# Output weights, input row norms and first convolution tap: a change of engine and of order in a gated DeltaNet and MLA kernel

## The chip, the cores and the metric

The kernel runs on one core of one Trainium2 chip. The metric is the device time of one execution in microseconds (us). Of several executions the median counts; two kernels are compared by executions that alternate on the same chip.

## What is computed

The reference is a streaming encoder with two layers. Layer A is a gated DeltaNet, layer B a latent attention (MLA). 1024 tokens of width 1024 come in, 16 meta tokens are put ahead of them, and both layers have 8 heads of width 128. The change touches layer A alone:

```python
def deltanet_layer(x, valid, g_norm, w_in, conv_w, a_log, dt_bias, o_gain, w_out):
    h = jnp.where(valid[None, :, None], rms_norm(x, g_norm), 0)
    z = h @ w_in
    qkv = jax.nn.silu(causal_dwconv(z[..., :2 * DN_KW + DN_VW], conv_w))   # 4 taps for each channel
    gate = z[..., 2 * DN_KW + DN_VW:2 * DN_KW + 2 * DN_VW]
...
    o = gated_delta_rule(to_chunks(q), to_chunks(k), to_chunks(v), gate_chunks(g), gate_chunks(beta))
    o = o.transpose(0, 2, 3, 1, 4).reshape(bsz, lp, DN_HEADS, DN_DV)
    o = rms_norm(o, o_gain) * jax.nn.silu(gate).reshape(bsz, lp, DN_HEADS, DN_DV)
    return x + o.reshape(bsz, lp, DN_VW) @ w_out
```

Shared keys and values, the attention layer and its output projection follow; they stay as they are.

## The kernel before

All products are split: an operand is rounded to the matmul's reduced fp32 (`hi`), the remainder is kept (`lo`), and three products (hi hi, hi lo, lo hi; the helper `mm3`, lines 93 to 95) make one. So each operand needs a rounding and a remainder. `split_w` does that for weights: the rounding on GpSimd (line 100, or line 103 with a gain) or VectorE, the remainder on VectorE (lines 101 and 104). `split_ps` does it for PSUM, with the rounding on ScalarE (lines 109 and 112).

The 1040 tokens go through layer A in three chunks of 272, 384 and 384 columns (`TOKC`). The stages that matter here:

Input. The first chunk comes transposed from memory (`x0`). For the other two, three row tiles of 128 tokens each are loaded (`xt`), squared on ScalarE with a sum for each row (`tok_norms`, into row tiles `xs`, of which there are 4), scaled on GpSimd by the inverse norm (line 292), transposed by TensorE (line 297) and split into `hT_hi` and `hT_lo`. Chunk 1 is squared early; chunk 2 is squared, scaled and transposed in its turn of the loop.

Projections. `conv_acts` makes one head's keys, values or queries: for each chunk 24 products of a chunk's width into one of two PSUM banks (`mm`), a copy to `z` on ScalarE (line 389), the first tap on GpSimd (line 391), three taps on VectorE (line 394), a SiLU on ScalarE. That is 24 heads' parts by 3 chunks. The tile for values (`vT`) has one buffer, that for queries two, that for keys four. In between, `key_prep` transposes keys (line 416) and squares them on ScalarE out of PSUM, masks gate tiles on GpSimd (line 448) for TensorE (line 450), and `query_prep` makes one-column products (line 494) and key-query products (line 502). `invert_blocks` is a long run on VectorE (lines 543 and 546), and the chunk scan follows.

Gates and output weights. For each head h the gate projection (three chunks, a SiLU each on ScalarE, stored to `gt_scr` for the first six heads) and the output weights of that head: a raw tile (`raw`, two buffers) is loaded and split by line 743 with the gain `og` for each row. Beside it the output norms are raised to a power on GpSimd (line 712, `output_norms`). The projection weights of the last eight heads are rounded on VectorE.

Every engine and SyncE's queue of transfers runs its own list of instructions in order and waits on semaphores. The order in each list is settled when the program is built, by priority in program order and by what is ready then; it can differ from the order of the text.

Of the kernel before, what the change touches and what calls it, by code (L numbers as in the profile page):

```python
# [16 lines left out]
F32 = mybir.dt.float32  # L17
# [33 lines left out]
def tools(tc):  # L51
# [45 lines left out]
    def split_w(raw, hi, lo, gain=None, eng=G):  # L97

        if gain is None:
            eng.tensor_scalar(out=hi, in0=raw, scalar1=1.0, scalar2=1.0, op0=ALU.mult, op1=ALU.mult)  # L100
            V.tensor_tensor(out=lo, in0=raw, in1=hi, op=ALU.subtract)  # L101
        else:
            G.tensor_scalar(out=hi, in0=raw, scalar1=gain, scalar2=1.0, op0=ALU.mult, op1=ALU.mult)  # L103
            return V.scalar_tensor_tensor(out=lo, in0=raw, scalar=gain, in1=hi, op0=ALU.mult, op1=ALU.subtract)  # L104

    def split_ps(ps, hi, lo, gain=None):
# [12 lines left out]
def body(ctx: ExitStack, tc: tile.TileContext, I, out):  # L119
# [63 lines left out]
    with ExitStack() as la:  # L183
# [51 lines left out]
        with ExitStack() as l0:  # L235
# [19 lines left out]
            def tok_norms(tiles):  # L255

                ss = xp.tile([P, 3], F32, tag="ss", name=nm("ss"), bufs=2)
                xss = [xp.tile([P, D], F32, tag="xs", name=nm("xs"), bufs=4) for _ in tiles]
                for i, t in enumerate(tiles):
                    act(xss[i], xts[t], AF.Square, accum_out=ss[:, i:i + 1])  # L260
                rsqrt(ss, ss, 1.0 / D, EPS)
                return ss, xss


            ps = bank("tr", [P, 512])[:, 0:W0]
# [19 lines left out]
            ready[order[1]] = load_w(order[1])  # L285
            V.tensor_tensor(out=gg, in0=col("kg"), in1=col("qg"), op=ALU.mult)
            V.tensor_scalar(out=gg, in0=gg, scalar1=QK ** -0.5, scalar2=None, op0=ALU.mult)
            for c, (a, b) in list(enumerate(TOKC))[1:]:
                tiles = [t for t in range(NT) if a <= tok(t)[0] < b]
                ss, xss = first if c == 1 else tok_norms(tiles)  # L290
                for i, t in enumerate(tiles):
                    G.tensor_scalar(out=xss[i], in0=xts[t], scalar1=ss[:, i:i + 1], scalar2=1.0,
                                    op0=ALU.mult, op1=ALU.mult)
                for kt in range(KT):
                    ps = bank("tr", [P, 512])
                    for i, xs in enumerate(xss):
                        TE.transpose(ps[:, P * i:P * i + P], xs[:, kt * P:(kt + 1) * P], ident)
                    split_ps(ps[:, 0:b - a], hT_hi[:, kt, a:b], hT_lo[:, kt, a:b], col("a", kt))
# [82 lines left out]
        def conv_acts(c0, tag, bufs):  # L381

            hi, lo = weights(c0)
            m = c0 // P
            z = zp.tile([P, 3 + L], F32, tag="z", name=nm("z"))
            y = kp.tile([P, L], F32, tag=tag, name=nm(tag), bufs=bufs)
            G.memset(z[:, 0:3], 0.0)
            for c, (a, b) in enumerate(TOKC):
                A.copy(z[:, 3 + a:3 + b], gemm_T(hi, lo, c))  # L389
                yc = y[:, a:b]  # L390
                G.tensor_scalar(out=yc, in0=z[:, a:b], scalar1=col("cw", m), scalar2=1.0,  # L391
                                op0=ALU.mult, op1=ALU.mult)
                for j in range(1, 4):
                    V.scalar_tensor_tensor(out=yc, in0=z[:, a + j:b + j], scalar=col("cw", 24 * j + m), in1=yc,  # L394
                                           op0=ALU.mult, op1=ALU.add)
                act(yc, yc, AF.Silu)
            return y
# [334 lines left out]
        with ExitStack() as lr:  # L732
            rp = lr.enter_context(tpool(name="wr", bufs=2))
            for h in range(H):
# [5 lines left out]
                    SY.dma_start(gt_scr[h * P:(h + 1) * P, :], z)  # L740
                raw = rp.tile([P, D], F32, tag="raw", name=nm("raw"))
                SY.dma_start(raw, I["a_w_out"][0, h * P:(h + 1) * P, :])
                last = split_w(raw, w_hi[:, h, :], w_lo[:, h, :], col("og"))
                if h > 1:
                    next(norms, None)
            for _ in norms:
# [754 lines left out]
```

## Time and profile before

| | us |
|---|---|
| three executions | 1347.64, 1343.96, 1349.01 |
| their median | 1347.64 |
| the profiled execution, its own time | 1343.6 |
| its span, from first to last instruction | 1341.9 |
| TensorE products busy in it | 1299.7 |
| TensorE's mean granted clock | 0.992 |

A row of the profile names engines as PE (TensorE products), PEld (its weight loads), DVE (VectorE), ACT (ScalarE), POOL (GpSimd), SP (SyncE). L391 is line 391 of the kernel. An instruction's idle time is that of its engine just before it, and the name behind the arrow is what ended it. Ends of TensorE's products are modelled: a product of 384 columns is drawn as 0.34 us, and the next one starts 0.18 us after it.

### The profile page before, as it was taken

Reading aid. Unit: us, or ns where it says so; the run is one execution under the profiler, and the core shown is the slowest. Engines: PE = TensorE matmul, PEld = TensorE weight load, DVE = VectorE, ACT = ScalarE, POOL = GpSimd, SP = SyncE. Lnnn points to the kernel's source line nnn. Section 1 sums busy time; section 2 is a strip of 40 time slices with the busy share of each in tenths; the row PEclk is TensorE's granted clock in tenths of the full one; section 3 lists DMA queues with packets and bytes.
Section 4 is the critical chain, followed back from the end, with each engine's and each line's share of the span. In section 5 each row is a group of like instructions: output and inputs, shape, how many; then the busy total and the mean of one; then the engine's idle time right before and its main releaser. Section 6 shows DMA issues by size and latency. Waiting matters only on the chain.

```text
span 1341.9 us, 24805 instructions
## 1 busy us (share of the span) xinstructions
PE 1299.7 (97%) x9047; PEld 1178.1 (88%) x9047; DVE 901.2 (67%) x2588; ACT 533.0 (40%) x1680; POOL 405.9 (30%) x677
## 2 busy tenths in 40 slices
PE   6999999999999999999999999998999999999998
PEld 5879989989998999996888798887999999998787
DVE  6679779968988884634553765224888878878321
ACT  5432343234225322211232343116778677776200
POOL 3353224323431320060101402212535436337100
PEclk9999999999999999999999999999999999999999
DMA  5111202111211113255541303311111101014443
GB/s 195 32 33 40 57 20 62 41 42 31 66 50 31 50 32 97 68 168 175 160 137 65 95 1 91 115 48 57 42 41 33 58 21 37 20 38 136 143 145 110
DMA packets 91676, 96.81 MB, mean 72 GB/s; under 512 B 27422, under 2 KB 72414, under 8 KB 91554
## 3 DMA queue, kind: packets, MB, share of 16 engines
q1 hardware_dynamic: 91554, 95.23, 22.8%
q8 instruction: 71, 1.16, 0.4%
q14 instruction: 51, 0.42, 0.1%
HBM read 68.19 MB, written 27.01 MB: 71 GB/s over the span
## 4 chain that ended last, share of the span: by engine, by line
PE 71%; DVE 9%; issue 5%; POOL 5%; ACT 4%; DMA 3%; SPq 0%; ACTq 0%; DVEq 0%; POOLq 0%
PE sc L95 6%; PE sc L94 6%; PE sc L93 6%; PE mm L93 6%; PE mm L94 6%; PE mm L95 6%; PE bd L93 5%; PE bd L95 4%; PE bd L94 4%; PE pt L1331 2%; PE tr L502 1%; PE sc L1284 1%; PE sc L1285 1%; DVE qT L394 1%; PE po L95 1%
## 5 line engine op out<-in xcount | busy, mean ns | idle before, releaser
L93 PE MATMUL mm<-hT_hi,whi 128*128 128x384 f32 (+1 forms) x768 | 256.6, 334 | 6.8 <-ACT hT_hi L283 4.3
L94 PE MATMUL mm<-hT_lo,whi 128*128 128x384 f32 (+1 forms) x768 | 256.6, 334 | 0.5 <-DVE hT_lo L284 0.5
L95 PE MATMUL mm<-hT_hi,wlo 128*128 128x384 f32 (+1 forms) x768 | 255.3, 332 | 0.7 <-DVE wlo L101 0.7
L93 PEld LDWEIGHTS mm<-hT_hi,whi 128*128 128x128 f32 x768 | 147.4, 192 | 9.4 <-issue 7.8
L95 PEld LDWEIGHTS mm<-hT_hi,wlo 128*128 128x128 f32 x768 | 147.6, 192 | 2.3 <-DVE wlo L101 1.1
L94 PEld LDWEIGHTS mm<-hT_lo,whi 128*128 128x128 f32 x768 | 147.1, 192 | 2.5 <-DVE hT_lo L284 1.0
L110 DVE TENSOR_TENSOR pTl<-pt,pTh 128x256 fp32r<-128x256 f32 (+2 forms) x112 | 54.9, 494 | 11.9 <-ACT pTh L109 10.4
L100 POOL TENSOR_SCALAR whi<-raw 128x512 fp32r<-128x512 f32 x48 | 37.4, 792 | 76.9 <-PE mm L94 71.2
L84 ACT ACTIVATE P<-P,mx 128x144 f32<-128x144 f32 (+3 forms) x64 | 50.6, 791 | 21.7 <-DVE mx L1289 19.2
L93 PE MATMUL sc<-wo_hi,oTh 128*128 128x512 f32 (+1 forms) x144 | 57.6, 400 | 0.6 <-ACT oTh L777 0.6
L95 PE MATMUL sc<-wo_hi,oTl 128*128 128x512 f32 (+1 forms) x144 | 57.2, 397 | 0.0
L94 PE MATMUL sc<-wo_lo,oTh 128*128 128x512 f32 (+1 forms) x144 | 57.0, 396 | 0.0
L389 ACT COPY z<-mm 128x384 f32<-128x384 f32 (+1 forms) x72 | 31.8, 442 | 56.7 <-PE mm L95 56.7
L394 DVE SCALAR_TENSOR_TENSOR kn<-z,pcol,kn 128x384 f32<-128x384 f32 (+1 forms) x72 | 41.0, 572 | 18.6 <-POOL kn L391 17.9
L109 ACT CAST pTh<-pt 128x256 fp32r<-128x256 f32 (+2 forms) x112 | 47.2, 426 | 14.2 <-PE pt L1331 7.2
L1302 POOL TENSOR_SCALAR P<-P,sl 128x144 f32<-128x144 f32 (+3 forms) x64 | 51.5, 806 | 3.7
L1300 POOL TENSOR_SCALAR Pe<-P,sl 128x128 f32<-128x128 f32 x64 | 29.5, 462 | 71.3 <-DVE sl L1297 55.2
L95 PE MATMUL sc<-h_hi,wlo 128*128 128x512 f32 x128 | 50.8, 397 | 0.0
L94 PE MATMUL sc<-h_lo,whi 128*128 128x512 f32 x128 | 50.6, 396 | 0.0
L93 PE MATMUL sc<-h_hi,whi 128*128 128x512 f32 x128 | 50.5, 395 | 0.0
L101 DVE TENSOR_TENSOR wlo<-raw,whi 128x512 fp32r<-128x512 f32 x64 | 46.0, 730 | 6.6 <-POOL whi L100 6.5
L104 DVE SCALAR_TENSOR_TENSOR wlo<-raw,pcol,whi 128x128 fp32r<-128x128 f32 x64 | 23.4, 428 | 40.0 <-POOL whi L103 40.0
(390 smaller groups left out, 3953.2 us busy)
## 6 DMA issues: line engine op xcount, KB each, us to landing
raw<-in_a_w_in SPq DMA_DIRECT2D x64, 256.0 KB
xt<-in_x SPq DMA_DIRECT2D x14, 512.0 KB
o_scr<-o SPq DMA_DIRECT2D x64, 64.0 KB
raw<-in_a_w_out SPq DMA_DIRECT2D x8, 512.0 KB
on<-o_scr SPq DMA_DIRECT2D x8, 512.0 KB
x_scr<-xt SPq DMA_DIRECT2D x8, 512.0 KB
raw<-in_b_w_in SPq DMA_DIRECT2D x8, 512.0 KB
gb_scr<-z SPq DMA_DIRECT2D x8, 512.0 KB
```

The costliest lines, as they stand in the source:

```text
L84: i = A.activation(out_ap, in_ap, func, **kw)
L93: TE.matmul(ps, ahi, bhi, start=first, stop=False)
L94: TE.matmul(ps, ahi, blo, start=False, stop=False)
L95: TE.matmul(ps, alo, bhi, start=False, stop=last)
L100: eng.tensor_scalar(out=hi, in0=raw, scalar1=1.0, scalar2=1.0, op0=ALU.mult, op1=ALU.mult)
L101: V.tensor_tensor(out=lo, in0=raw, in1=hi, op=ALU.subtract)
L109: A.copy(hi, ps)
L110: V.tensor_tensor(out=lo, in0=ps, in1=hi, op=ALU.subtract)
L389: A.copy(z[:, 3 + a:3 + b], gemm_T(hi, lo, c))
L394: V.scalar_tensor_tensor(out=yc, in0=z[:, a + j:b + j], scalar=col("cw", 24 * j + m), in1=yc, op0=ALU.mult, op1=ALU.add)
L1300: G.tensor_scalar(out=Pe, in0=Pm[:, None, 0:NM].broadcast_to([P, E8, NM]), scalar1=s, scalar2=1.0, op0=ALU.mult, op1=ALU.mult)
L1302: G.tensor_scalar(out=Pm[:, 0:n], in0=Pm[:, 0:n], scalar1=s, scalar2=1.0, op0=ALU.mult, op1=ALU.mult)
```

## The change

Three edits. `split_w` with a gain takes the engine that it is given: the eight output weight tiles are rounded by ScalarE (`A.mul` with the gain as a scale for each partition) in place of GpSimd; the remainder stays on VectorE, and other callers with a gain keep GpSimd. The norms and the scaling of both later input chunks are issued ahead of the loop over their transposes, with 6 row tiles in place of 4. The first tap of the convolution is an `A.mul` on ScalarE in place of a multiplication on GpSimd.

```diff
--- before.py
+++ after.py
@@ -100,7 +100,10 @@
             eng.tensor_scalar(out=hi, in0=raw, scalar1=1.0, scalar2=1.0, op0=ALU.mult, op1=ALU.mult)
             V.tensor_tensor(out=lo, in0=raw, in1=hi, op=ALU.subtract)
         else:
-            G.tensor_scalar(out=hi, in0=raw, scalar1=gain, scalar2=1.0, op0=ALU.mult, op1=ALU.mult)
+            if eng is A:
+                A.mul(hi, raw, gain)
+            else:
+                G.tensor_scalar(out=hi, in0=raw, scalar1=gain, scalar2=1.0, op0=ALU.mult, op1=ALU.mult)
             return V.scalar_tensor_tensor(out=lo, in0=raw, scalar=gain, in1=hi, op0=ALU.mult, op1=ALU.subtract)
 
     def split_ps(ps, hi, lo, gain=None):
@@ -255,11 +258,17 @@
             def tok_norms(tiles):
 
                 ss = xp.tile([P, 3], F32, tag="ss", name=nm("ss"), bufs=2)
-                xss = [xp.tile([P, D], F32, tag="xs", name=nm("xs"), bufs=4) for _ in tiles]
+                xss = [xp.tile([P, D], F32, tag="xs", name=nm("xs"), bufs=6) for _ in tiles]
                 for i, t in enumerate(tiles):
                     act(xss[i], xts[t], AF.Square, accum_out=ss[:, i:i + 1])
                 rsqrt(ss, ss, 1.0 / D, EPS)
                 return ss, xss
+
+            def scaled(tiles, ss, xss):
+                for i, t in enumerate(tiles):
+                    G.tensor_scalar(out=xss[i], in0=xts[t], scalar1=ss[:, i:i + 1], scalar2=1.0,
+                                    op0=ALU.mult, op1=ALU.mult)
+                return xss
 
 
             ps = bank("tr", [P, 512])[:, 0:W0]
@@ -285,12 +294,9 @@
             ready[order[1]] = load_w(order[1])
             V.tensor_tensor(out=gg, in0=col("kg"), in1=col("qg"), op=ALU.mult)
             V.tensor_scalar(out=gg, in0=gg, scalar1=QK ** -0.5, scalar2=None, op0=ALU.mult)
+            rows = {1: scaled(range(2, 5), *first), 2: scaled(range(5, 8), *tok_norms(range(5, 8)))}
             for c, (a, b) in list(enumerate(TOKC))[1:]:
-                tiles = [t for t in range(NT) if a <= tok(t)[0] < b]
-                ss, xss = first if c == 1 else tok_norms(tiles)
-                for i, t in enumerate(tiles):
-                    G.tensor_scalar(out=xss[i], in0=xts[t], scalar1=ss[:, i:i + 1], scalar2=1.0,
-                                    op0=ALU.mult, op1=ALU.mult)
+                xss = rows[c]
                 for kt in range(KT):
                     ps = bank("tr", [P, 512])
                     for i, xs in enumerate(xss):
@@ -388,8 +394,7 @@
             for c, (a, b) in enumerate(TOKC):
                 A.copy(z[:, 3 + a:3 + b], gemm_T(hi, lo, c))
                 yc = y[:, a:b]
-                G.tensor_scalar(out=yc, in0=z[:, a:b], scalar1=col("cw", m), scalar2=1.0,
-                                op0=ALU.mult, op1=ALU.mult)
+                A.mul(yc, z[:, a:b], col("cw", m))
                 for j in range(1, 4):
                     V.scalar_tensor_tensor(out=yc, in0=z[:, a + j:b + j], scalar=col("cw", 24 * j + m), in1=yc,
                                            op0=ALU.mult, op1=ALU.add)
@@ -740,7 +745,7 @@
                     SY.dma_start(gt_scr[h * P:(h + 1) * P, :], z)
                 raw = rp.tile([P, D], F32, tag="raw", name=nm("raw"))
                 SY.dma_start(raw, I["a_w_out"][0, h * P:(h + 1) * P, :])
-                last = split_w(raw, w_hi[:, h, :], w_lo[:, h, :], col("og"))
+                last = split_w(raw, w_hi[:, h, :], w_lo[:, h, :], col("og"), A)
                 if h > 1:
                     next(norms, None)
             for _ in norms:
```

## Rows read from the trace of the kernel before

**Rows 1.** The page's first part: busy time of each engine over the whole span, its share, and the count of its instructions; PE is TensorE's products, PEld its weight loads.

```profile
PE 1299.7 (97%) x9047; PEld 1178.1 (88%) x9047; DVE 901.2 (67%) x2588; ACT 533.0 (40%) x1680; POOL 405.9 (30%) x677
```

**Rows 2.** The table of 20 us windows: stretch, length, then for each engine its busy time and instructions in it, TensorE's granted clock (1.00 is 2.4 GHz, 0.50 is 1.2 GHz), the transfers' share and rate.

```profile
460.00:480.00 20.00, 20.00 (x135) 19.77 (x134) 18.76 (x51) 5.49 (x15) 7.63 (x7) 1.00 0.12 37
...
600.00:620.00 20.00, 17.78 (x108) 17.27 (x107) 9.27 (x18) 2.27 (x5) 4.07 (x3) 1.00 0.54 172
```

**Rows 3.** The timeline of GpSimd (POOL) in the stage of the gate projections and output weights, 478 to 632 us: start, duration, engine, line, operation, tiles, shape, count, and in brackets the idle time before it and what ended that.

```profile
571.71 12.96 POOL L712 TENSOR_TENSOR ro<-oss,half 128x8 f32<-128x8 f32 x8 [34.78 <-DVE oss L710]
...
584.64 2.23 POOL L103 TENSOR_SCALAR wo_hi<-raw,pcol 128x1024 fp32r<-128x1024 f32 x2
...
591.32 1.12 POOL L103 TENSOR_SCALAR wo_hi<-raw,pcol 128x1024 fp32r<-128x1024 f32 x1 [4.45 <-DMA raw<-in_a_w_out]
```

**Rows 4.** The same stretch on SyncE's queue: issues of transfers.

```profile
568.28 0.33 SPq L742 DMA_DIRECT2D raw<-in_a_w_out  x1
...
587.97 1.52 SPq L742 DMA_DIRECT2D raw<-in_a_w_out  x2
...
589.54 0.43 SPq L204 DMA_DIRECT2D raw<-in_a_w_in  x1
```

**Rows 5.** The timeline of VectorE (DVE) at the end of that stretch. Line 100 rounds a head's projection weights, line 104 is the remainder of the output weights.

```profile
595.99 0.76 DVE L100 TENSOR_SCALAR whi<-raw 128x512 fp32r<-128x512 f32 x2
...
608.98 1.28 DVE L104 SCALAR_TENSOR_TENSOR wo_lo<-raw,pcol,wo_hi 128x1024 fp32r<-128x1024 f32 x1 [1.02 <-POOL wo_hi L103]
...
610.19 0.76 DVE L100 TENSOR_SCALAR whi<-raw 128x512 fp32r<-128x512 f32 x2
```

**Rows 6.** The timeline of ScalarE (ACT) in that stretch: the SiLU that empties each bank of the gate products (first chunk 272 columns, the others 384). The idle time before it is the wait for TensorE's last product of the chunk.

```profile
587.55 0.40 ACT L84 ACTIVATE zg<-mm 128x272 f32<-128x272 f32 x1 [2.60 <-PE mm L95]
...
600.48 0.40 ACT L84 ACTIVATE glast<-mm 128x272 f32<-128x272 f32 x1 [4.03 <-PE mm L95]
...
608.93 0.49 ACT L84 ACTIVATE glast<-mm 128x384 f32<-128x384 f32 x1 [3.73 <-PE mm L95]
...
614.68 0.40 ACT L84 ACTIVATE glast<-mm 128x272 f32<-128x272 f32 x1 [5.26 <-PE mm L95]
```

**Rows 7.** Groups of instructions by line and shape on ScalarE, 20 to 495 us: line, engine, operation, tiles, shapes, count, then the group's busy time and the mean ns of one, then idle time before.

```profile
L112 ACT ACTIVATE hT_hi<-tr,pcol 128x384 fp32r<-128x384 f32 x16 | 8.7, 579 | 5.5 <-PE tr L297 5.1
...
L84 ACT ACTIVATE xs<-xt 128x1024 f32<-128x1024 f32 x2 | 2.1, 1053 | 0.0
```

**Rows 8.** The timeline of ScalarE and of GpSimd, 14 to 62 us: squares (line 84) and scalings (line 292) of the last input chunk, and the rounding of the second head's weights (line 100).

```profile
16.05 1.05 ACT L84 ACTIVATE xs<-xt 128x1024 f32<-128x1024 f32 x1
...
28.41 1.05 ACT L84 ACTIVATE xs<-xt 128x1024 f32<-128x1024 f32 x1
...
21.14 1.20 POOL L100 TENSOR_SCALAR whi<-raw 128x512 fp32r<-128x512 f32 x2
...
31.19 3.31 POOL L292 TENSOR_SCALAR xs<-xt,ss 128x1024 f32<-128x1024 f32 x3 [8.85 <-ACT ny L84]
```

**Rows 9.** The timeline of TensorE, 31 to 37 us: transposes of the last input chunk (line 297).

```profile
33.46 0.55 PE L297 MATMUL tr<-ident,xs 128*128 128x128 f32 x3 [0.19 <-POOL xs L292]
...
34.55 0.55 PE L297 MATMUL tr<-ident,xs 128*128 128x128 f32 x3 [0.55 <-POOL xs L292]
...
35.55 0.36 PE L311 MATMUL fin<-hT_hi,wab 128*32 128x384 f32 x1 [0.45 <-ACT hT_hi L112]
```

**Rows 10.** The instructions of line 391 (the first tap): duration in ns as minimum, median and maximum, first and last start in us, shapes; the last row is from the list of who waited for them, in us and times.

```profile
L391 POOL TENSOR_SCALAR kn<-z,pcol x24: 484/587/1532, 34.5 to 400.5; 128x384 f32<-128x384 f32 x16, 128x272 f32<-128x272 f32 x8
...
L391 POOL TENSOR_SCALAR qT<-z,pcol x24: 496/1136/3717, 102.7 to 488.0; 128x384 f32<-128x384 f32 x16, 128x272 f32<-128x272 f32 x8
...
  DVE kn L394: 17.9, 12
```

**Rows 11.** Who waited for whom over the whole span: us in total, times, the longest.

```profile
PEld tr L416 <- ACT junk L84: 6.3, 27, 0.7
...
PEld tr L450 <- POOL gm L448: 5.2, 19, 0.6
...
PE tr L506 <- DVE epsq L496: 0.9, 2, 0.6
...
POOL vT L391 <- PE tr L521: 4.4, 2, 2.7
```

**Rows 12.** The timeline of ScalarE in the key preparation: a copy of products from PSUM (line 389) and a square of the transposed keys (line 84) at its first stretch, and the copy in the last one. The two copies are the first and the last of ten that start between the transposes of line 416 or within 1 us ahead of them.

```profile
59.10 0.48 ACT L389 COPY z<-mm 128x384 f32<-128x384 f32 x1 [0.54 <-PE mm L95]
...
60.27 0.28 ACT L84 ACTIVATE junk<-tr 128x128 bf16<-128x128 f32 x1 [0.42 <-PE tr L416]
...
427.99 0.47 ACT L389 COPY z<-mm 128x384 f32<-128x384 f32 x1
```

**Rows 13.** Two windows, columns as in rows 2: the first and the last of the five stretches from 100 to 500 us in which TensorE's granted clock is below 1.00 (the second one is a 20 us window that holds such a stretch).

```profile
125.60:129.00 3.40, 3.04 (x16) 2.74 (x15) 3.33 (x10) 1.63 (x4) 0.68 (x1) 0.50 0.00 0
...
480.00:500.00 20.00, 19.44 (x136) 18.76 (x135) 17.04 (x44) 5.20 (x12) 5.24 (x3) 0.94 0.09 27
```

**Rows 14.** The timeline of TensorE around two of the query preparations: the one-column products (line 494) and the sixteen key-query products (line 502).

```profile
123.01 2.08 PE L494 MATMUL tr<-ones,sq 128*16 128x1 f32 x18
...
124.95 3.17 PE L502 MATMUL tr<-qT,kn 128*128 128x128 f32 x16
...
369.63 2.03 PE L502 MATMUL tr<-qT,kn 128*128 128x128 f32 x16
```

## The prediction, made before the changed kernel was run

> **What bounds the kernel now.** I read the page's busy table first: TensorE is busy 97% of the span with products, and beside its own weight loads nothing is above 67% [rows 1]. Then the 20 us windows: TensorE is full in most of the stage of the input projections (20.00 of 20 us at 460), and the widest hole in what the change touches after the start is where the output weights are prepared (17.78 of 20 us at 600) [rows 2]. So work taken off GpSimd is worth nothing by itself. The 405.9 us that GpSimd is busy are no bound; a part of the change can only be worth the TensorE holes that it fills, less those that it opens. The third view is therefore who TensorE waits for in each of the three stages touched, and what stands on the two engines that trade work.
>
> **Output weights on ScalarE.** The change takes eight roundings of 1024 columns off GpSimd and puts eight of the same size on ScalarE. On GpSimd they stand behind the powers of the output norms: those run from 571.71 for 12.96 us, so the first rounding starts at 584.64 although its raw tile was asked for at 568.28 [rows 3, 4]. The landing takes 591.32 - 587.97 = 3.35 us where nothing else delays it, so the first tile was there by about 572. From then on the eight go in a ring of two raw tiles: landing, rounding, remainder on VectorE, next landing. VectorE does its queue in order, and the last two heads' projection weights (line 100) stand behind these remainders: at 595.99, and at 610.19, right behind a remainder that began at 608.98 [rows 5]. TensorE waits for them. ScalarE's SiLU shows by how much: before that of a head's first chunk it idles 2.60 us until the products are done when the weights were ready, and 4.03 and 5.26 us for the last two heads [rows 6]. That is 1.43 + 2.66 = 4.1 us of TensorE.
> ScalarE has only one SiLU of 0.4 to 0.5 us every 3 to 4 us there [rows 6]. A 1024 column pass on it takes 1.05 us [rows 7], against 1.12 on GpSimd [rows 3], so the pass itself gains nothing; what changes is that the ring starts some 12 us earlier, at about 572. The last remainder would then end near 597, before the last head's weights are wanted at about 608. I take the whole 4.1 us. The other end is below nothing: ScalarE now waits for the landings, and the SiLUs that empty TensorE's two banks stand behind it. One stop of 3.35 + 1.05 = 4.4 us against the 3.73 + 0.49 = 4.2 us in which the next chunk fills the other bank [rows 6] costs 0.2 us; six stops cost about 1 us.
>
> **Norms and scaling ahead of the transposes.** Nothing is added. The three squares and three scalings of the last input chunk move ahead, with six row tiles where there were four. Now one of these squares runs at 16.05 and the last only at 28.41, since it waits for a row tile; GpSimd scales from 31.19 [rows 8]. TensorE meets this at 33.46 to 35.55, where it idles 0.19 + 0.55 us for the scalings and 0.45 us for the cast of what was transposed late [rows 9]. That is 1.2 us, and I take it: GpSimd is free from 22.34, so the scalings could end before 27. At the other end the two squares, 1.05 us each, come between the casts at the start that feed TensorE's first products; they cost up to 2.1 us if each delays a cast that TensorE waits for. Neither the cast nor the square changes its length, and ScalarE idles between the last casts, so I keep that end for the range only. The rounding of the second head's weights, queued near the scalings on GpSimd, ends at 22.34 now (21.14 + 1.20); behind three scalings of 1.1 us it would end near 26, while the first head's products still have a chunk to go after the transposes at 35.
>
> **First tap on ScalarE.** It takes 72 passes off GpSimd (24 each for keys, values and queries; medians 0.59 for keys and, beside VectorE's inversion, 1.14 us for queries with one of 3.72) [rows 10] and puts 72 on ScalarE: 0.58 us for 384 columns by the nearest row, a scaled cast [rows 7], or 48 x 0.58 + 24 x 0.5 = 40 us over 470 us (0.5 for 272 columns, as the SiLU takes 0.09 less for them than for 384 [rows 6]). VectorE idled 17.9 us for the keys' taps [rows 10], mostly under a full TensorE. What TensorE itself got from that is the two waits for the query norms, 0.9 us [rows 11], both behind a late tap on VectorE's queue; I take 0.9 us as gained (the other end is 0).
> Against it stands the key preparation. There TensorE transposes and ScalarE squares in turn, and TensorE's weight loads already waited 6.3 us in 27 times for the squares [rows 11]. ScalarE idles 0.42 us before such a square [rows 12], so a tap of 0.58 that lands in one gap pushes the next square by 0.16 us, and one that finds no gap by 0.58. Ten of the 72 copies from PSUM stand in these eight stretches, the first at 59.10, the last at 427.99 [rows 12]. The ends are 10 x 0.16 = 1.6 and 10 x 0.58 = 5.8 us; I take eight times 0.3 = 2.4 us, nearer to the short one, since gaps of that size are what ScalarE has most of there.
>
> **Sum.** 4.1 + 1.2 + 0.9 - 2.4 = 3.8 us less. Against the profiled execution (1343.6 us, span 1341.9) this is 1339.8. That execution is at the fast end of what was timed: the three others have a median of 1347.64. So I give 1347.6 - 3.8 = 1343.8, rounded to 1344.
>
> **The rivals.**
> *More than the holes (chance 0.26).* TensorE's clock falls to half at 125.60 to 129.00, right behind 18 one-column matmuls; the sixteen products there take 3.17 us where sixteen of the same kind at 369.63 take 2.03 [rows 13, 14]. A fall costs 1.7 us (3.4 us at half rate, 1.2 in place of 2.4 GHz), and five of them lie in this stage, the last in the window at 480 [rows 13]. If the new order loses two, that is 3.4 us. The masked gate tiles, for which TensorE's loads waited 5.2 us [rows 11], could also come faster when GpSimd is emptier; half is 2.6 us. Together 3.8 + 3.4 + 2.6 = 9.8 us: 1338. For it: GpSimd's lengths vary widely now (0.50 to 3.72 us for the queries' taps) [rows 10], which looks like contention. Against it: the waits for the gate tiles stand between GpSimd passes of that group, not behind taps, and clock falls can be added as well as lost. The Trainium skill ("GPSIMD Engine Reference", Specifications) says that GpSimd shares its SBUF interfaces with VectorE and that they contend in VectorE instructions with two SBUF inputs; by that rule the gain is this rival's, and the spread of the taps agrees. The Trainium skill ("TensorE: Matmul & The Clock Gate", What's actually happening) has the clock follow how busy the array was lately; the fall behind the one-column matmuls agrees.
> *The wait only changes engine (chance 0.17).* The output weights' ring is set by landings and two raw tiles, not by the powers: a landing of 3.35 and passes of 1.1 and 1.3 make 5.7 us for two tiles, and if the order on SyncE puts the landings behind the stores of the gates, the last remainders still end past 608. Then the 4.1 us stay: 0.3 us lost, 1347.9, no change. For it: two of the landings were asked for only at 587.97 and a projection weight's at 589.54 right behind [rows 4]. Against it: the two at 587.97 waited for the first remainders, behind a rounding that began only at 584.64 [rows 3].
> *ScalarE's queue holds the banks (chance 0.10), slower.* The value tile has one buffer, so the next value head's tap waits until the last one's transposes have read it; on GpSimd such taps waited 4.4 us in two times [rows 11], at no cost. On ScalarE, copies from PSUM stand behind them. It decides from the point at which a stop exceeds the 4.2 us that the other bank covers. If the eight value heads lose 1.7 us each (a wait of 2.7, a copy and two taps, and a SiLU that is held in turn come to about 6 us), that is 13.6 - 6.2 = 7.4 us more with the gains of 4.1, 1.2 and 0.9 kept: 1355. For it, the Trainium skill ("ScalarE: Activation LUTs", Rules for kernel authors) sends multiplications to VectorE and not to ScalarE; the trace has a VectorE near full in places, so it bears the rule out only where ScalarE is in turn with TensorE. Against it: ScalarE is busy about a quarter to a half of these windows, and a copy that is ready can stand ahead of a tap that is not.
>
> **How the numbers follow.** The forecast has 0.47. About 0.5% (6.7 us) is what a measurement of this kernel can tell from no change, since the three runs before span 5 us. Faster by more than that: 0.24 of the first rival and 0.10 of the forecast (if two costs come out at their good ends). Slower: nearly all of the third, 0.09, and 0.01 of the forecast. That leaves 0.56 within 0.5%. The range leaves out the third rival's time and the far end of the first: 1334 to 1352. The top also takes in the bounds: no gain from the weights, 2.1 lost to the squares and 2.4 lost to the taps give 1352.
>
> **What would show it.** Steps right: no longer step than about 3.1 us to the 272 column chunks of the last two gate heads; the roundings of the output weights spread from about 573 to 596; the last chunk's scalings begin before 24; waits of the transposes for the squares up by 1 to 4 us; DVE idle for the first tap gone. Wrong: SiLUs on ScalarE waiting behind a landing; copies from PSUM a chunk late behind a tap; a different count of clock falls that outweighs all this; or TensorE's own order so changed that the holes lie elsewhere.

## The result, and the profile after

The changed kernel takes 1336.01 us (median of 16 runs, 1332.93 to 1342.46) against 1344.76 us of the kernel before (16 runs, 1337.62 to 1353.36) on the same chips. The ratio is 0.9941, 95% interval 0.9920 to 0.9962: 7.9 us faster, between 5.1 and 10.8. The forecast was 1344 within 1334 to 1352, from a sum of 3.8 us gained. The sign was right and the range held; the gain is twice the sum. Of the 8 us between 1344 and 1336.0, 2.9 are not the change at all but the base: the prediction set out from three executions with a median of 1347.64, and 16 give 1344.76. One execution of the kernel before, taken beside the experiments below, lasted 4627 us, and is left out as slow.

The profiled execution of the changed kernel took 1339.67 us (span 1338.0, mean granted clock 0.986). The page's busy table answers to [rows 1]: 79 us have left GpSimd, 48 have come to ScalarE, and VectorE, which was given nothing and lost nothing, is busy 8 us less.

```profile
PE 1301.6 (97%) x9047; PEld 1181.1 (88%) x9047; DVE 893.4 (67%) x2588; ACT 581.4 (43%) x1760; POOL 327.2 (24%) x597
```

**Output weights.** The timeline of ScalarE in the stage of the gates, to be read beside [rows 3, 5, 6]: line 104 is the rounding that came over, line 84 the SiLU.

```profile
572.69 1.15 ACT L104 ACTIVATE wo_hi<-raw,pcol 128x1024 fp32r<-128x1024 f32 x1
...
579.09 1.15 ACT L104 ACTIVATE wo_hi<-raw,pcol 128x1024 fp32r<-128x1024 f32 x1 [2.31 <-DMA raw<-in_a_w_out]
...
586.88 0.40 ACT L84 ACTIVATE zg<-mm 128x272 f32<-128x272 f32 x1 [0.81 <-PE mm L95]
...
595.37 1.16 ACT L104 ACTIVATE wo_hi<-raw,pcol 128x1024 fp32r<-128x1024 f32 x1 [1.91 <-DMA raw<-in_a_w_out]
596.43 0.47 ACT L84 ACTIVATE zg<-mm 128x384 f32<-128x384 f32 x1
598.31 0.40 ACT L84 ACTIVATE glast<-mm 128x272 f32<-128x272 f32 x1 [1.41 <-PE mm L95]
...
609.80 0.40 ACT L84 ACTIVATE glast<-mm 128x272 f32<-128x272 f32 x1 [2.54 <-PE mm L95]
```

The eight roundings run from 572.69 to 596.5; the first one no longer stands behind GpSimd's powers. Ahead of the last two heads' first SiLU ScalarE idles 1.41 and 2.54 us, where it idled 4.03 and 5.26. Some roundings do wait for a landing (2.31, 1.91 us), and the SiLU at 596.43 starts late behind one, without idle time; the next chunk still follows at 598.31. From the SiLU of the first chunk two heads back to that of the last head it is 609.80 - 586.88 = 22.9 us, against 614.68 - 587.55 = 27.1 before [rows 6]: 4.2 us less.

**Norms and scaling.** The last step of the last chunk's norms on VectorE (line 182), GpSimd's scalings, TensorE's transposes, and then ScalarE in the first key preparation, which answers to [rows 12]: copy, tap (line 397) and squares.

```profile
25.63 0.14 DVE L182 SCALAR_TENSOR_TENSOR ss<-nt,ny 128x3 f32<-128x3 f32 x1
...
25.94 3.32 POOL L269 TENSOR_SCALAR xs<-xt,ss 128x1024 f32<-128x1024 f32 x3 [3.09 <-DMA raw<-in_a_w_in]
...
29.31 0.66 PE L303 MATMUL tr<-ident,xs 128*128 128x128 f32 x4 [0.24 <-POOL xs L269]
...
58.61 0.48 ACT L395 COPY z<-mm 128x384 f32<-128x384 f32 x1 [0.57 <-PE mm L95]
...
59.24 0.61 ACT L397 ACTIVATE kn<-z,pcol 128x384 f32<-128x384 f32 x1
59.77 0.28 ACT L84 ACTIVATE junk<-tr 128x128 bf16<-128x128 f32 x1
...
60.56 0.28 ACT L84 ACTIVATE junk<-tr 128x128 bf16<-128x128 f32 x1 [0.42 <-PE tr L421]
```

The scalings start at 25.94 and not at 31.19 [rows 8], right after the norms that they read (25.63 + 0.14; the landing that the bracket names had long been there). The three squares end at 20.5, but the steps from them to the norms stand on VectorE between the remainders of other tiles. But the transposes have moved forward too, and wait for the scalings nearly as long as before. TensorE's waits from 20 to 46 us, first of the kernel before, then of the changed one:

```profile
PE tr L297 <- POOL xs L292: 1.1, 3, 0.5
PE fin L311 <- ACT hT_hi L112: 0.5, 1, 0.5
```

```profile
PE tr L303 <- POOL xs L269: 1.0, 3, 0.5
```

Only the wait for the cast is gone. At 58.61 against 59.10, 0.5 us is left of it.

**First tap.** Who waited for whom, to be read beside [rows 11]; the last row is from the stretch 55 to 500 us alone.

```profile
PEld tr L455 <- POOL gm L453: 5.0, 17, 0.7
PEld tr L421 <- ACT junk L84: 5.0, 23, 0.3
...
DVE kn L399 <- ACT kn L397: 19.4, 11, 2.8
```

The transposes wait for ScalarE's squares 5.0 us and not 6.3, though ScalarE has 72 more passes: in the rows above the tap at 59.24 pushes one square to 59.77, and by the next, at 60.56, ScalarE again idles 0.42 us for TensorE; the gate tiles are as late as they were (5.2); and VectorE waits for the keys' first tap no less than it did (19.4 us against 17.4 in the same stretch; the 17.9 of [rows 10] are of the whole span), now for ScalarE. The two waits of 0.9 us for the query norms [rows 11] are gone. What has changed on VectorE is the length of its passes. Groups by line from 55 to 500 us, first of the kernel before, then of the changed one; `tmp` and `M` are the inversion of the query blocks, which the change does not touch:

```profile
L546 DVE TENSOR_TENSOR M<-M,tmp 66x31 f32<-66x31 f32 (+15 forms) x116 | 44.5, 384 | 0.6
L543 DVE TENSOR_TENSOR tmp<-M 66x31 f32<-66x31 f32 (+15 forms) x116 | 43.6, 376 | 0.6
L394 DVE SCALAR_TENSOR_TENSOR vT<-z,pcol,vT 128x384 f32<-128x384 f32 (+1 forms) x72 | 43.0, 602 | 1.5 <-POOL vT L391 1.3
```

```profile
L399 DVE SCALAR_TENSOR_TENSOR vT<-z,pcol,vT 128x384 f32<-128x384 f32 (+1 forms) x72 | 41.2, 580 | 1.6 <-ACT vT L397 1.4
...
L551 DVE TENSOR_TENSOR M<-M,tmp 66x31 f32<-66x31 f32 (+15 forms) x115 | 40.5, 352 | 0.8
L548 DVE TENSOR_TENSOR tmp<-M 66x31 f32<-66x31 f32 (+15 forms) x115 | 40.5, 352 | 0.7
```

**The clock.** In the windows of the changed kernel where TensorE's granted clock is 0.50 (columns as in [rows 2]), two of eight between 100 and 1300 us:

```profile
366.30:369.70 3.40, 3.40 (x18) 3.14 (x18) 3.40 (x9) 1.10 (x3) 0.10 (x1) 0.50 0.22 77
...
407.30:417.50 10.20, 10.20 (x59) 9.02 (x59) 4.59 (x14) 3.95 (x17) 0.51 (x1) 0.50 0.01 2
```

The first follows 18 one-column products at 363.54, as the one at 125.60 did before [rows 13, 14]. The mean granted clock of this execution, 0.986 against 0.992, makes up to 1338.0 x 0.006 = 8 us more that the clock took. So two profiles alone don't tell what the parts are worth, and the runs had to.

### The profile page after: what moved, and what is told of

Read it like the earlier page. It is cut to its first block, busy times and chain, and to the rows that moved or that the text cites. A ratio compares the mean times of both kernels' runs of the same rounds, so it can differ in the third digit from the quotient of the medians.

```text
span 1338.0 us, 24787 instructions
## 1 busy us (share of the span) xinstructions
PE 1301.6 (97%) x9047; PEld 1181.1 (88%) x9047; DVE 893.4 (67%) x2588; ACT 581.4 (43%) x1760; POOL 327.2 (24%) x597
## 4 chain that ended last, share of the span: by engine, by line
PE 83%; DVE 6%; ACT 3%; issue 3%; POOL 2%; DMA 1%; SPq 0%; DVEq 0%; POOLq 0%; ACTq 0%
PE mm L93 9%; PE mm L94 9%; PE mm L95 9%; PE sc L95 6%; PE sc L94 6%; PE sc L93 6%; PE bd L93 5%; PE bd L95 4%; PE bd L94 4%; PE pt L1336 2%; PE tr L507 2%; PE ch L639 1%; PE tr L499 1%; PE ch L649 1%; PE ch L635 1%
## 5 line engine op out<-in xcount | busy, mean ns | idle before, releaser
L100 POOL TENSOR_SCALAR whi<-raw 128x512 fp32r<-128x512 f32 x48 | 34.4, 733 | 171.4 <-PE mm L94 136.7
L113 DVE TENSOR_TENSOR pTl<-pt,pTh 128x256 fp32r<-128x256 f32 (+2 forms) x112 | 54.9, 494 | 10.2 <-ACT pTh L112 8.8
L399 DVE SCALAR_TENSOR_TENSOR kn<-z,pcol,kn 128x384 f32<-128x384 f32 (+1 forms) x72 | 41.5, 576 | 22.9 <-ACT kn L397 22.1
L93 PE MATMUL sc<-kn_hi,qn_hi 128*128 128x272 f32 (+3 forms) x160 | 48.5, 305 | 2.0 <-DVE mx L1294 1.5
```

What stands on the lines that cost most here:

```text
L93: TE.matmul(ps, ahi, bhi, start=first, stop=False)
L113: V.tensor_tensor(out=lo, in0=ps, in1=hi, op=ALU.subtract)
```

## The experiments

Each timed run lists its time and its mean granted clock. Each row of the kernel before stands above the kernels that shared its chip and its runs; kernels below different rows ran on different chips. The column time x clock is the mean over a kernel's runs of that product, an estimate of the time at full clock. It over-corrects where the clock is low while TensorE waits anyway, and the runs show by how much: among the runs of one kernel (216 runs of 16 kernels and groups, the 16 of the result among them) 0.001 less of mean clock goes with 0.90 us more, and not with the 1.34 that the product takes. The last column uses that slope: the mean time, brought to one clock, less that of the kernel before in the same group, with a 95% interval of 0.9 to 1.8 us either way.

| kernel | median us | ratio to before (95%) | mean clock | time x clock | us against before at one clock |
|---|---|---|---|---|---|
| before (35 runs) | 1343.19 | | 0.9919 | 1332.7 | |
| wo_only (12) | 1341.39 | 0.9987 (0.9969 to 1.0004) | 0.9889 | 1326.9 | -4.5 |
| xs_only (12) | 1344.94 | 1.0014 (0.9992 to 1.0036) | 0.9907 | 1332.2 | +0.1 |
| tap_only (12) | 1344.01 | 1.0003 (0.9980 to 1.0027) | 0.9870 | 1327.1 | -3.4 |
| pow_last (12) | 1341.64 | 0.9991 (0.9972 to 1.0011) | 0.9890 | 1327.1 | -4.3 |
| before (25) | 1344.59 | | 0.9907 | 1332.2 | |
| all_again (9) | 1334.92 | 0.9925 (0.9896 to 0.9955) | 0.9892 | 1321.2 | -10.4 |
| no_weights (12) | 1342.60 | 0.9981 (0.9963 to 1.0000) | 0.9871 | 1326.1 | -4.5 |
| no_norms (6) | 1335.12 | 0.9914 (0.9893 to 0.9935) | 0.9898 | 1321.7 | -10.2 |
| no_tap (12) | 1341.16 | 0.9978 (0.9953 to 1.0002) | 0.9867 | 1324.3 | -6.1 |
| before (20) | 1344.34 | | 0.9902 | 1331.4 | |
| idle_pass (8) | 1336.95 | 0.9933 (0.9908 to 0.9957) | 0.9908 | 1324.6 | -7.2 |
| tap_on_vector (12) | 1339.09 | 0.9960 (0.9936 to 0.9983) | 0.9862 | 1320.9 | -8.9 |
| tap_keys_only (7) | 1335.89 | 0.9927 (0.9898 to 0.9956) | 0.9926 | 1326.4 | -6.2 |
| gate_ring3 (6) | 1332.67 | 0.9900 (0.9869 to 0.9932) | 0.9890 | 1318.5 | -12.6 |

**Each part alone, and the cause of the weights by itself.** The first three kernels take one part of the diff each: the roundings (lines 103 and 743), the norms' order and their two tiles more (lines 258 and 288), the tap (line 391). The fourth leaves the roundings on GpSimd and puts the powers behind them (cut; `rounded` is a list of the eight roundings, kept by `split_w`):

```diff
-                if h > 1:
-                    next(norms, None)
-            for _ in norms:
-                pass
+            with tc.issue_after(rounded[-1].ins):
+                for _ in norms:
+                    pass
```

Weights alone: 

> The output weights' edit alone, on the kernel before. If the last two gate heads waited for the ring of roundings (the prediction's term), the time falls by about 4.1 us (ratio 0.997), the SiLU of the last two gate heads' first chunks idles about 2.6 us in place of 4.03 and 5.26, and nothing ahead of 560 us differs from before. If the wait only changes engine, the time stays within 1 us and the idle times of these two SiLUs stay above 4 us. If the whole 8 us of the change lie here, the ratio is about 0.994.

Norms alone: 

> The norms and scaling alone, on the kernel before. By the prediction 1.2 us less (ratio 0.999): the waits of TensorE for the last chunk's scalings go. By what the changed kernel's trace shows (TensorE's transposes stand earlier too, and still wait 0.29 and 0.40 us for the scalings), 0.5 us or less, which can't be told from nothing in the time; then the end of the first head's products in the trace tells it. A loss of up to 2 us if the early squares hold up the first casts.

Tap alone: 

> The first tap on ScalarE alone, on the kernel before. By the prediction's terms 1.5 us more (2.4 lost in the key preparation, 0.9 gained at the query norms; ratio 1.001), with TensorE's loads for the key transposes waiting longer for the squares than the 6.3 us of before. By the rival that the tap brings what the prediction missed, 3 to 4 us less (ratio 0.997), with these waits no longer than before. If clock falls make the difference, the time moves by 1.7 us for each fall more or less in its trace.

Powers behind the roundings: 

> The kernel before, with the output norms' powers put behind the eight roundings in GpSimd's order; the roundings stay on GpSimd. If what held the ring was the place behind the powers, this brings the same 4.1 us as the output weights' edit (ratio 0.997), with the roundings beginning at about 572. If GpSimd itself is too slow for them (1.12 us against 1.15 on ScalarE, or the load on VectorE's remainders), less than half of that comes. If the powers then end too late for the first output tile, TensorE's first transposes of that stage wait for them and the gain shrinks by that wait.

No part alone differs from the kernel before by more than its interval. The product of the three ratios is 1.0004, and together they make 0.9941 (0.9925 below): in the time they don't add. GpSimd in pow_last, and below it ScalarE there:

```profile
571.59 1.12 POOL L105 TENSOR_SCALAR wo_hi<-raw,pcol 128x1024 fp32r<-128x1024 f32 x1 [62.76 <-DVE oss L712]
...
597.69 14.71 POOL L714 TENSOR_TENSOR ro<-oss,half 128x8 f32<-128x8 f32 x9
...
598.74 0.40 ACT L84 ACTIVATE glast<-mm 128x272 f32<-128x272 f32 x1 [2.54 <-PE mm L95]
...
610.22 0.40 ACT L84 ACTIVATE glast<-mm 128x272 f32<-128x272 f32 x1 [2.54 <-PE mm L95]
```

With the rounding still on GpSimd both waits of the last heads are gone, as in the changed kernel, so the powers ahead of the ring were the cause and not the engine. In wo_only they are gone as well (1.08 and 2.54 us). Both kernels gain at one clock what these waits cost (4.5 and 4.3 us), and hide most of it in the time behind a lower clock. Tap_only shows the other reason why the parts don't add. ScalarE, then the table of windows over the same stretch:

```profile
582.55 0.40 ACT L84 ACTIVATE zg<-mm 128x272 f32<-128x272 f32 x1 [2.59 <-PE mm L95]
...
600.86 0.40 ACT L84 ACTIVATE glast<-mm 128x272 f32<-128x272 f32 x1 [9.42 <-PE mm L95]
...
612.71 0.40 ACT L84 ACTIVATE glast<-mm 128x272 f32<-128x272 f32 x1 [2.75 <-PE mm L95]
```

```profile
591.20:594.20 3.00, 0.42 (x2) 0.30 (x2) 2.19 (x4) 0.24 (x1) 1.52 (x2) 1.00 0.43 164
594.20:601.00 6.80, 5.60 (x25) 5.53 (x25) 4.29 (x4) 0.14 (x1) 1.79 (x2) 0.50 0.94 304
```

The tap had brought the heads forward by 5.0 us (582.55 against 587.55, [rows 6]; both traces have five stretches of 3.4 us at 1.2 GHz ahead of that, so the clock has no part in it). But the output weights' ring did not come forward as far, and line 100's weights behind it start only 2.8 us earlier than before [rows 5]:

```profile
593.21 0.76 DVE L100 TENSOR_SCALAR whi<-raw 128x512 fp32r<-128x512 f32 x2
```

TensorE stands nearly empty for 3 us, and then runs at 1.2 GHz for 6.8 us. At the last head 2.0 of the 5.0 us are left (612.71 against 614.68). The waits for the squares are 5.0 us here too, so its expectation's rival holds in that, and not in the time.

**One part left out.** Each kernel is the changed one less one hunk; all_again is the changed one itself.

The whole change: 

> The whole change once more, beside the leave-one-out kernels. Each timed run lists its time and its mean granted clock; us x clock is the time it would have had at full clock (net), the rest is what the clock took. In the runs so far the kernel before has net 1332.7 and 10.9 us for the clock, the weights alone 1326.9 and 14.9, the tap alone 1327.1 and 17.5, the norms alone 1332.2 and 12.6, the whole change 1322.9 and 13.5 (on other chips). Theory A (the parts add in net time, and each kernel draws its own number of clock falls): net 11 to 12 us under before, 2 to 4 us more for the clock, about 8 us faster. Theory B (the parts need each other; the whole change was lucky in its chips): 0 to 3 us faster here.

Without the weights: 

> Norms ahead and tap on ScalarE, output weights as before. Theory A: net 6.0 us under before (5.5 + 0.5), 5.8 over the whole change; the idle times ahead of the SiLUs of the last two gate heads are back (4.0 and 5.3 us). Theory B: within 2 us of the whole change or of before, with no such step in net time.

Without the norms: 

> Output weights and tap, norms as before. Theory A: net 11.3 us under before and 0.5 over the whole change, so the same time as the whole change within what can be measured, unless the order draws other clock falls. Theory B (the norms make the other two count): net near before, 6 us or more slower than the whole change.

Without the tap: 

> Output weights and norms, the first tap on GpSimd as before. Theory A: net 6.3 us under before, 5.5 over the whole change; the waits of the transposes for the squares of the key preparation are back at 4.7 us (3.0 with the tap on ScalarE). If the tap's rival price of the prediction (2.4 us lost to the squares) held, this kernel would be 2 us faster than the whole change.

The whole change is 10 us faster here (0.9925 of 1344.59). Left out, the weights cost 1342.60 - 1334.92 = 7.7 us and the tap 6.2; the norms 0.2, nothing that can be measured. In no_weights the long stop is there again (ScalarE idle 9.67 us ahead of that SiLU, then 2.79, not the 4.0 and 5.3 expected):

```profile
596.96 0.40 ACT L84 ACTIVATE glast<-mm 128x272 f32<-128x272 f32 x1 [9.67 <-PE mm L95]
```

```profile
587.00:590.00 3.00, 0.08 (x1) 0.11 (x1) 1.84 (x3) 0.29 (x1) 1.70 (x2) 0.99 0.49 173
590.00:596.80 6.80, 5.91 (x25) 5.59 (x26) 4.64 (x5) 0.00 (x0) 2.14 (x2) 0.50 0.87 301
```

So theory A holds in time x clock: over the eight combinations the weights bring 4.9 to 7.9 us, the tap 3.1 to 6.1, the norms 0.5 to 2.6. At one clock the three parts alone make 7.7 of the whole change's 10.4 us. Of theory B one half holds in the time itself, that parts need each other (weights and tap, not the norms); the other, that the whole change was lucky, fell. The stop for the weights is 4.2 us where the heads come late, and 7.4 where the tap has brought them forward: in no_weights it is 608.69 - 578.40 = 30.3 us from the SiLU of the first chunk two heads back to that of the last head, against 22.9 in the changed kernel, and in tap_only 612.71 - 582.55 = 30.2. The 7.7 measured for the weights are near that. In no_tap the transposes wait 6.3 us in 27 times for the squares, as in [rows 11] (the 4.7 and 3.0 us of the expectations stand in no trace; they are 6.3 and 5.0), and the kernel is slower: the price of 2.4 us that the prediction set on the tap was a gain.

**What of the tap makes the gain, and one step more.** Edits to the changed kernel, one each: a GpSimd pass over the same data into a tile that nobody reads; the tap on VectorE; the tap on ScalarE for keys alone; a ring of three gate tiles.

```diff
                 A.mul(yc, z[:, a:b], col("cw", m))
+                idle = zp.tile([P, 384], F32, tag="idle", name=nm("idle"), bufs=1)[:, 0:b - a]
+                G.tensor_scalar(out=idle, in0=z[:, a:b], scalar1=col("cw", m), scalar2=1.0, op0=ALU.mult, op1=ALU.mult)
```

```diff
-                A.mul(yc, z[:, a:b], col("cw", m))
+                V.tensor_scalar(out=yc, in0=z[:, a:b], scalar1=col("cw", m), scalar2=None, op0=ALU.mult)
```

```diff
-                A.mul(yc, z[:, a:b], col("cw", m))
+                if tag == "kn":
+                    A.mul(yc, z[:, a:b], col("cw", m))
+                else:
+                    G.tensor_scalar(out=yc, in0=z[:, a:b], scalar1=col("cw", m), scalar2=1.0,
+                                    op0=ALU.mult, op1=ALU.mult)
```

```diff
-                    gs = [bp.tile([P, 2, P], F32R, tag=f"g{y}", name=nm("gm")) for y in range(2)]
+                    gs = [bp.tile([P, 2, P], F32R, tag="gs", name=nm("gm"), bufs=3) for y in range(2)]
```

Idle pass: 

> The whole change, with GpSimd also doing every first tap again into a tile that nobody reads: the queue of the first tap stays on ScalarE, GpSimd's passes of that size come back. So far the whole change has net 1321.2 us (time x granted clock) and no_tap 1324.3; VectorE's inversion passes (tmp and M) take 351 and 352 ns there, 376 and 384 in the kernel before. Contention theory (what the tap's move gives is GpSimd's absence beside VectorE): the inversion passes go back to about 375 to 385 ns and net rises by 3 to 5 us. Queue theory (it is the place of the tap, on ScalarE right behind the copy that it reads): net within 1 us of the whole change, whatever the passes' length.

Tap on VectorE: 

> The whole change with the first tap on VectorE in place of ScalarE, so neither GpSimd nor ScalarE has it: 72 passes more on VectorE's queue, which has the other three taps and the inversion. Contention theory alone: as fast as the whole change, since GpSimd is as empty. Queue theory: VectorE's taps stand behind the inversion's passes, so the query's and the keys' first taps come late; net 2 to 4 us over the whole change. The Trainium skill (ScalarE: Activation LUTs, Rules for kernel authors) sends a multiplication to VectorE rather than ScalarE; by that rule alone this kernel is the faster one.

Keys alone: 

> The whole change with the first tap on ScalarE for the keys alone (24 of 72 passes); values and queries have it on GpSimd as before. If the gain of the tap lies in the key preparation (the keys' end comes a microsecond earlier, the waits of the transposes for the squares fall from 4.7 to 3.0 us), net is within 1 us of the whole change and these waits stay at 3.0. If it lies with the queries and values (the query norms late behind a late tap, the inversion slowed by GpSimd), net goes back by 2 us or more and the squares' waits stay at 3.0 all the same.

Ring of three: 

> The whole change with a ring of three masked gate tiles in place of one buffer each for the high and the low part. TensorE's weight loads waited 5.2 us for these tiles before and 5.0 with the whole change, though GpSimd has 70 us less to do: so GpSimd's load is not what makes them late. If it is the single buffer (GpSimd must wait until TensorE has read the last tile), these waits fall by half or more and net by 2 to 4 us, faster than the whole change. If it is the length of the two passes themselves (0.40 to 0.85 us each for two products of 0.39), nothing changes.

VectorE's inversion, 55 to 500 us, in idle_pass:

```profile
L550 DVE TENSOR_TENSOR tmp<-M 66x31 f32<-66x31 f32 (+15 forms) x118 | 45.4, 384 | 1.2 <-POOL M L546 0.5
L553 DVE TENSOR_TENSOR M<-M,tmp 66x31 f32<-66x31 f32 (+15 forms) x118 | 44.3, 375 | 0.8
```

and in tap_on_vector:

```profile
L548 DVE TENSOR_TENSOR tmp<-M 66x31 f32<-66x31 f32 (+15 forms) x116 | 40.3, 348 | 0.1
L551 DVE TENSOR_TENSOR M<-M,tmp 66x31 f32<-66x31 f32 (+15 forms) x116 | 39.9, 344 | 0.1
```

The lengths follow GpSimd's passes whoever has the tap: 384 and 375 ns with them, 348 and 344 without, and 369 and 367 in tap_keys_only, where two thirds of them are back. That GpSimd slows VectorE beside it is shown. TensorE feels it. From 60 to 475 us (columns as in [rows 2]) before, after, idle_pass and tap_on_vector, in this order:

```profile
60.00:475.00 415.00, 410.29 (x3277) 381.15 (x3278) 348.27 (x1008) 145.29 (x499) 140.40 (x222) 0.98 0.17 45
```

```profile
60.00:475.00 415.00, 412.50 (x3263) 384.02 (x3263) 340.19 (x1003) 179.36 (x561) 78.45 (x158) 0.97 0.17 45
```

```profile
60.00:475.00 415.00, 410.88 (x3294) 382.35 (x3294) 351.95 (x1010) 180.54 (x564) 160.20 (x222) 0.98 0.16 45
```

```profile
60.00:475.00 415.00, 412.37 (x3289) 384.38 (x3289) 357.54 (x1070) 146.52 (x501) 125.37 (x158) 0.98 0.16 45
```

TensorE stands without a product for 415 - 410.29 = 4.7 us with the taps on GpSimd (4.4 to 5.2 in the five kernels of that kind), 2.5 in the changed kernel and 2.6 with the tap on VectorE. With the idle pass it is 4.1 again, and as much in tap_keys_only. So most of these 2.2 us is contention; one wait of 1.0 us for the query norms, as before, is among what the idle pass brings back.

In time x clock the idle pass costs 1324.6 - 1321.2 = 3.4 us and the tap on VectorE nothing (1320.9), so the queue theory, which had it the other way round, isn't borne out. Keys alone on ScalarE gives back 5.2 us there, more than no_tap, which gives back the whole tap (3.1): that is the over-correction, since this kernel's clock was the highest of all (0.9926). At one clock the idle pass gives back 3.2 us, the tap on VectorE 1.5 and keys alone 4.2, of the 4.3 that no_tap does (each by 2 to 2.5 either way, and across two chips). So the gain is not the keys' alone (the waits for the squares there are 5.3 us, and 5.4 in idle_pass), and contention is a large part of it. How large is open: the idle pass is a little more than what was taken away (1.29 us a pass on the mean against 0.97), and it also reads `z`, and ScalarE's copies and taps waited for GpSimd three times (5.8 us; the trace puts no wait of TensorE's products down to these copies). In the time itself these three are less clear: idle_pass (0.9933) and tap_keys_only (0.9927) can't be told from the whole change, since they lost less to the clock; tap_on_vector (0.9960) lost more. How much of the tap's gain reaches the time is left to clock falls that no run here steers.

In gate_ring3 the waits for the gate tiles fall from 5.0 us in 17 times to

```profile
PEld tr L455 <- POOL gm L453: 4.0, 12, 0.7
```

and time x clock by 2.7 us (2.2 at one clock). Its median, 1332.67, is the lowest of all, but its interval overlaps that of the whole change. The waits fell by a fifth and not by half, and that fall is not the ring's by any proof: with the old tiles they are 3.9 us in 14 times in tap_on_vector and 4.2 in 14 in tap_keys_only. That a ring of three helps is not shown.

## Why the prediction was right in sign and half in size

- **Weights, 4.1 us: right, mechanism and size** (4.2 in the trace of the changed kernel; in pow_last, by the same two SiLUs, 610.22 - 587.30 = 22.9 against 27.1, 4.2 as well; 4.5 and 4.3 us at one clock in wo_only and pow_last). Also right: the first rounding at about 572, the last remainder near 597 (it starts at 596.98), SiLUs behind a landing without a price. The rival that the wait only changes engine fell with pow_last. What the sum missed: the term was priced with the heads where they stood. The tap brings them forward, and the stop for the weights then costs 7.4.
- **Norms, 1.2 us: less than half of it came.** 0.5 us in the trace, nothing in the time. The scalings came 5 us earlier, but the term left the transposes where they stood: they came earlier too and waited for the scalings 1.0 us in place of 1.1. Only the wait for the cast (0.45) went. "The last chunk's scalings begin before 24" failed (25.94): the step had counted squares and scalings, and not the steps between them on VectorE, 5.1 us from the last square to the norms (20.5 to 25.6).
- **Tap, 0.9 - 2.4 = 1.5 us lost: wrong in sign.** This is the step that failed. Moving the tap was worth 5.0 us by the gates in tap_only, 3.4 to 4.3 at one clock and, left out, 6.2 in the time. The 0.9 us for the query norms did come (no such wait is left in the changed kernel, and one of 1.0 is back with the idle pass), but it was the only gain counted; that GpSimd's passes lengthen VectorE's was put at nothing. The waits for the squares, expected to grow by 1 to 4 us, fell from 6.3 to 5.0, and the longest from 0.7 to 0.3. The tap shown at 59.24 does push a square, but the gap of 0.42 us behind it takes that up. Nor do these waits follow ScalarE's load: in tap_on_vector, which spares ScalarE the 72 passes, they are 6.6 us in 30 times. "DVE idle for the first tap gone" failed too: 19.4 us, since VectorE waits there for a copy that itself waits for TensorE's products, and then for the tap, as it did when GpSimd had it (for the pass before 152.31: copy at 151.14, tap at 151.66).
- **The rival *More than the holes*** named 9.8 us and was near in time, but by luck: neither of the two terms that it added came. The gate tiles came no faster (5.0 against 5.2 us), and the clock took no less (0.9899 as mean of the 16 runs, against 0.9902 to 0.9919 of the kernel before). Its ground, that GpSimd's spread of tap lengths looks like contention, was the right one. The Trainium skill ("GPSIMD Engine Reference", Specifications) has GpSimd share its SBUF interfaces with VectorE, in contention for instructions with two SBUF inputs. The inversion's passes have two, and agree: 376 and 384 ns with GpSimd's taps, 352 without.
- **The banks behind ScalarE's queue (slower):** did not happen. Value taps did wait on ScalarE for their tile, 4.3 us in four times, but the longest was 2.0 us, below the 4.2 that the other bank covers. The Trainium skill ("ScalarE: Activation LUTs", Rules for kernel authors) sends a multiplication to VectorE; tap_on_vector is as fast by time x clock (1320.9 against 1321.2), 1.5 us behind at one clock, and not faster in time (1339.09 against 1334.92), so no run here bears the rule out.
- **The sum, 3.8 us:** the sign came from the weights. With the tap's sign wrong, that 1336.0 still lies within the range, 2 us from its lower end, is luck.
- **Open:** which waits of TensorE hold the tap's 5 us one by one (the 2.2 us without a product and the 1.3 fewer behind squares are what the traces name), and what decides a kernel's number of clock falls. Wo_only and pow_last lack 4.2 us of waits, and gave back some 2.7 us of it by a mean clock lower by 0.003.

## What to carry to other kernels

Price a part of a change with the other parts in place: a stage that gets faster runs into the next late resource, and what that costs is no longer what the old trace shows. An engine that is no bound can still be in the way of one beside it; look whether the untouched passes of its neighbour vary in length, and give it an idle pass to see what it costs. Where a kernel's time moves with the clock by as much as with the change, take the granted clock of each run beside the time before a part is called worthless, and take the price of the clock from the spread of the runs: time x clock overstated it by half here, enough to make two thirds of the taps look worth more than all of them.

## What the runs showed that was not expected

The same program draws other clock falls in another execution. At 407 us the changed kernel ran 10.2 us at 1.2 GHz in one profiled execution; in the other (all_again), at the same place, one third of that:

```profile
407.00:410.40 3.40, 3.40 (x19) 2.84 (x18) 2.72 (x10) 1.61 (x7) 0.00 (x0) 0.54 0.00 0
410.50:417.50 7.00, 7.00 (x65) 6.21 (x64) 3.77 (x14) 4.30 (x20) 0.52 (x1) 0.99 0.02 5
```

The places recur (124, 141, 366, 383 and 407 us in both), the lengths don't. And a stop of TensorE can cost twice: 3 us nearly empty in tap_only and no_weights, and then 6.8 us at half clock in both.
